# RMSNorm with SiLU on one core: rstd and gamma in one pass by rows, an even split of the squares, and no alignment of VectorE's code

## The chip, the cores and the metric

The kernel runs on one core of a Trainium2 chip. The metric is the device time of one execution in microseconds (us), as a median over runs. One more execution is taken by the hardware profiler; from it come the profile page and the trace.

## The reference

```python
x: (8, 1024, 2048) float32;  gamma: (2048,) float32;  eps = 1e-5
rms = sqrt(mean(x ** 2, axis=-1, keepdims=True) + eps)
out = gamma * x / rms
return out * (1 / (1 + exp(-out)))        # SiLU
```

So there are 8192 rows of 2048 numbers. Each row has one statistic (its root mean square), and every element is read once and written once: 67.11 MB in, 67.11 MB out.

## The kernel before

The rows are cut into 16 blocks of 512 rows. A block lies in SBUF as 128 partitions with J = 4 rows of d = 2048 each, so a block is a tile of 128x8192 float32, 4.19 MB. Six such blocks (BUFS) form a ring, `xt`; everything is computed in place in the ring. A block is loaded by one DMA that ScalarE issues (`load`, L70; blocks 4 and 5 come in one double load, L74), and stored by one DMA that SyncE issues (`store`, L146). The load of block b+6 has to wait until block b's store has emptied the buffer. That wait stands in ScalarE's own instruction stream, in front of what ScalarE does next. TensorE is used once at the start, to spread gamma over the 128 partitions.

The order of all instructions is written out by hand (`tc.manual_schedule()`). The steps of a block b are:

- `squares_scalar(b)` (L91) and `squares_vector(b)` (L100): sums of squares of the four rows. The first `share(b)` rows go to ScalarE, the others to VectorE. The share is two, but one in blocks 4, 6, 8, 10 and 12. Between ScalarE's first and second square (or behind its only one) stands a load.
- `root(b)` (L113, ScalarE) and `invert(b)` (L119, VectorE): from the sums to 1/rms (`rstd`). From block 2 on, blocks go in pairs, and one root and one reciprocal serve both (128x8). Each root costs two loads of ScalarE's function table, one for the root and one to go back to SiLU.
- `multiply(b)`: in blocks 0 and 1 (`SINGLE`), one scalar-tensor-tensor per row, which multiplies by `rstd` and gamma in one pass (L133). In all later blocks (`plain`), one tensor-tensor over the whole block that multiplies by gamma alone (L130). That one doesn't need the statistic, so it is issued right behind the block's squares.
- `silu(b)`: in blocks 0 and 1, two instructions of two rows each (L142). In later blocks, four instructions of one row, which take `rstd` as their per-partition scale (L139). Then the store.

In the main loop, for b = 2, 4, ... 14, ScalarE and VectorE do in this order: the squares of b+1 (with the load of b+3), root and reciprocal for b and b+1, the multiply of b+1, SiLU and store of b, the squares of b+2 (with the load of b+4), the multiply of b+2, SiLU and store of b+1.

At the very start VectorE has an `addr_align` to a multiple of 128 instruction slots (L151). It moves the code that follows to the next such slot, and VectorE branches over the hole.

Of the kernel before, what the change touches and what calls it, by code (L numbers as in the profile page):

```python
# [7 lines left out]
ACT = mybir.ActivationFunctionType  # L8
# [3 lines left out]
@with_exitstack  # L12
def kernel(
    ctx: ExitStack,
    tc: tile.TileContext,
    x: bass.AP,
    gamma: bass.AP,
    eps: bass.AP,
    out: bass.AP,
):  # L20

    nc = tc.nc
    P = nc.NUM_PARTITIONS
    f32 = mybir.dt.float32
    x2 = x.flatten_outer_dims()
    o2 = out.flatten_outer_dims()  # L30
    n, d = x2.shape
    J = 4
    BUFS = 6
    SLOTS = 128
    SINGLE = 2
    SHARE = {4: 1, 6: 1, 8: 1, 10: 1, 12: 1}
    nblk = n // (P * J)
    PAIRS = (4,)

    def view(t, b):  # L40

        for q in PAIRS:
            if b in (q, q + 1):
                both = t[q * P * J:(q + 2) * P * J, :].rearrange("(p j) d -> p (j d)", p=P, j=2 * J)
                return both[:, (b - q) * J * d:(b - q + 1) * J * d]
        return t[b * P * J:(b + 1) * P * J, :].rearrange("(p j) d -> p (j d)", p=P, j=J)

    singles = ctx.enter_context(tc.tile_pool(name="singles", bufs=1))
    small = ctx.enter_context(tc.tile_pool(name="small", bufs=2))
    psum = ctx.enter_context(tc.tile_pool(name="psum", bufs=1, space=bass.MemoryType.PSUM))  # L50

    Q = 4
    w = d // Q
    g = singles.tile([P, d], f32)
    eps_t = singles.tile([P, 1], f32)
    ones = singles.tile([P, P], f32)
    junk_a = psum.tile([P, d], f32, name="junk_a")
    junk_v = psum.tile([P, d], f32, name="junk_v")
    ring = singles.tile([P, BUFS * J * d], f32, name="xt")
    sss, rmss, rstds = {}, {}, {}  # L60

    def rows(b, j, k):
        at = (b % BUFS) * J + j
        return ring[:, at * d:(at + k) * d]

    def row(b, j):
        return rows(b, j, 1)

    def load(b):
        nc.scalar.dma_start(out=rows(b, 0, J), in_=view(x2, b))  # L70

    def load_pair(b):
        both = x2[b * P * J:(b + 2) * P * J, :].rearrange("(p j) d -> p (j d)", p=P, j=2 * J)
        nc.scalar.dma_start(out=rows(b, 0, 2 * J), in_=both)  # L74

    def group(b):

        return [b] if b < SINGLE else [b, b + 1]

    def sums(b):  # L80
        if b not in sss:
            k = len(group(b))
            t = small.tile([P, k * J], f32, name="ss")
            for i, m in enumerate(group(b)):
                sss[m] = (t, i * J)
        return sss[b]

    def squares_scalar(b, loads=()):
        t, at = sums(b)
        for j in range(share(b)):  # L90
            nc.scalar.activation(out=junk_a, in_=row(b, j), func=ACT.Square,  # L91
                                 accum_out=t[:, at + j:at + j + 1])
            if j == 0:
                for s in loads:
                    load(s)

    def squares_vector(b):
        t, at = sums(b)
        for j in range(share(b), J):
            nc.vector.tensor_tensor_reduce(  # L100
                out=junk_v, in0=row(b, j), in1=row(b, j), scale=1.0, scalar=0.0,
                op0=ALU.mult, op1=ALU.add, accum_out=t[:, at + j:at + j + 1])

    def share(b):
        return SHARE.get(b, 2)

    def plain(b):
        return b >= SINGLE

    def root(b):  # L110
        k = len(group(b)) * J
        rms = small.tile([P, k], f32, name="rms")
        nc.scalar.activation(out=rms, in_=sss[b][0], func=ACT.Sqrt, scale=1.0 / d, bias=eps_t)  # L113
        rmss[b] = rms

    def invert(b):
        k = len(group(b)) * J
        rstd = small.tile([P, k], f32, name="rstd")
        nc.vector.reciprocal(out=rstd, in_=rmss.pop(b))  # L119
        for i, m in enumerate(group(b)):  # L120
            rstds[m] = (rstd, i * J)

    def scale(b, j):
        t, at = rstds[b]
        return t[:, at + j:at + j + 1]

    def multiply(b):
        if plain(b):
            whole = rows(b, 0, J).rearrange("p (j d) -> p j d", j=J)
            nc.vector.tensor_mul(out=whole, in0=whole, in1=g.unsqueeze(1).to_broadcast([P, J, d]))  # L130
            return
        for j in range(J):
            nc.vector.scalar_tensor_tensor(out=row(b, j), in0=row(b, j), scalar=scale(b, j),  # L133
                                           in1=g, op0=ALU.mult, op1=ALU.mult)

    def silu(b):
        if plain(b):
            for j in range(J):
                nc.scalar.activation(out=row(b, j), in_=row(b, j), func=ACT.Silu, scale=scale(b, j))  # L139
        else:  # L140
            for h in range(0, J, 2):
                nc.scalar.activation(out=rows(b, h, 2), in_=rows(b, h, 2), func=ACT.Silu)  # L142
        store(b)

    def store(b):
        nc.sync.dma_start(out=view(o2, b), in_=rows(b, 0, J))  # L146

    with tc.manual_schedule():

        load(0)  # L150
        nc.vector.addr_align(SLOTS, max_nops=0)  # L151
        nc.vector.memset(ones, 1.0)  # L152
        nc.vector.memset(eps_t, float(eps))
        nc.scalar.activation(out=junk_a[:, 0:1], in_=ones[:, 0:1], func=ACT.Square)  # L154
        nc.sync.dma_start(out=g[0:1, :], in_=bass.AP(tensor=gamma.tensor, offset=gamma.offset, ap=[[d, 1], [1, d]]))
        for c in range(Q):
            cols = slice(c * w, (c + 1) * w)
            nc.tensor.matmul(junk_v[:, cols], ones[0:1, :], g[0:1, cols], start=True, stop=True)  # L158
        load(1)
        nc.vector.tensor_copy(out=g, in_=junk_v)  # L160
        nc.scalar.copy(out=junk_a[:, 0:1], in_=junk_v[:, d - 1:d])  # L161
        for b in range(2, PAIRS[0]):
            load(b)
        for b in PAIRS:
            load_pair(b)


        squares_scalar(0)
        squares_vector(0)
        root(0)  # L170
        invert(0)
        multiply(0)
        squares_scalar(1)
        silu(0)
        squares_vector(1)
        root(1)
        invert(1)
        multiply(1)
        squares_scalar(2)
        silu(1)  # L180
        squares_vector(2)
        multiply(2)

        for b in range(SINGLE, nblk, 2):
            squares_scalar(b + 1, [b + 3] if BUFS <= b + 1 and b + 3 < nblk else [])
            squares_vector(b + 1)
            root(b)
            invert(b)  # L190
            multiply(b + 1)
            silu(b)
            ahead = b + 2
            if ahead < nblk:
                if b == SINGLE:
                    load(BUFS)
                    silu(b + 1)
                    squares_scalar(ahead, [BUFS + 1])
                    squares_vector(ahead)
                    multiply(ahead)  # L200
                    continue
                squares_scalar(ahead, [ahead + 2] if ahead + 2 < nblk else [])
                squares_vector(ahead)
                multiply(ahead)
            silu(b + 1)


# [33 lines left out]
```

## Time and profile before

| | |
|---|---|
| median of 3 runs | 318.05 us (317.35 to 318.18) |
| the profiled execution | 317.71 us, of which the span of the profile is 315.3 us |
| VectorE (DVE) busy | 229.3 us, 73% of the span, 108 instructions |
| ScalarE (ACT) busy | 201.6 us, 64% of the span, 144 instructions |
| DMA | 134.24 MB, 426 GB/s over the span |

The span runs from the first to the last instruction of the program; 2.4 us of the execution lie around it. In the lines of the profile, `out<-in` names what an instruction writes and reads, `x` is a count, then come busy time and mean duration in nanoseconds, and then the idle time of the engine just ahead of them with what ended it. The DMA row gives the busy share of the 16 DMA engines in 40 slices of the span, in tenths. Queue q10 carries the loads, q1 the stores and the gamma row, q14 the engines' own code.

### The profile page before, as it was taken

To read this page: it belongs to the slowest core of one execution; us is meant where nothing else is said; L and a number is where in the kernel's file an instruction comes from. 1 tells how busy PE (TensorE), PEld (TensorE's weight loads), DVE (VectorE), ACT (ScalarE), POOL (GpSimd) and SP (SyncE) were. 2 spreads that over 40 slices of the span, in tenths; PEclk is the share of its full clock that TensorE was granted. 3 is DMA by queue.
4 is the path that set the end of the run, shared out by engine and by line. 5 is a ranking of instruction groups with operands and counts; after the bars stand their busy time and mean duration, and the time that the engine had idled before them with its cause. 6 is when DMAs were issued, how large, how long until landed. Compare 5 with 4: busy or idle time off the path is not lost.

```text
span 315.3 us, 398 instructions
## 1 busy us (share of the span) xinstructions
PE 7.2 (2%) x8; PEld 2.5 (1%) x8; DVE 229.3 (73%) x108; ACT 201.6 (64%) x144; POOL 0.2 (0%) x4
## 2 busy tenths in 40 slices
PE   6200000000000000000000000000000000000000
PEld 2000000000000000000000000000000000000000
DVE  0579599979797999799933999349992599891000
ACT  1249999079854993793808948098470999699100
POOL 0000000000000000000000000000000000000000
DMA  8999999999999999999999999999999999999996
GB/s 331 412 453 416 437 412 399 470 461 399 416 449 417 449 416 449 424 441 432 432 437 428 445 420 449 416 449 416 449 416 453 412 453 412 453 412 461 403 466 270
DMA packets 4468, 134.24 MB, mean 426 GB/s; under 512 B 497, under 2 KB 497, under 8 KB 497
## 3 DMA queue, kind: packets, MB, share of 16 engines
q10 hardware_dynamic: 2160, 67.11, 49.7%
q1 hardware_dynamic: 2306, 67.12, 49.3%
q14 instruction: 2, 0.02, 0.0%
HBM read 67.12 MB, written 67.11 MB: 426 GB/s over the span
## 4 chain that ended last, share of the span: by engine, by line
DMA 51%; ACT 21%; DVE 17%; issue 2%; ACTq 1%; DVEq 0%
DMA out_dram<-xt 44%; ACT xt L139 13%; DVE xt L130 8%; DMA xt<-in_x_dram 7%; DVE junk_v L100 6%; DVE xt L133 3%; ACT L113 2%; ACT junk_a L91 2%; ACT xt L142 2%; ACT L139 1%; ACTq L236 1%; ACT rms L113 0%; ACTq L70 0%; ACT L142 0%; DVE ss L100 0%
## 5 line engine op out<-in xcount | busy, mean ns | idle before, releaser
L130 DVE TENSOR_TENSOR xt<-xt,g 128x8192 f32<-128x8192 f32 x14 | 121.3, 8666 | 2.6 <-ACT junk_a L91 2.0
L139 ACT ACTIVATE xt<-xt,rstd 128x2048 f32<-128x2048 f32 x56 | 107.3, 1989 | 14.7 <-DMA out_dram<-xt 14.6
L100 DVE CUSTOM_DVE_ANT_0 junk_v<-xt 128x2048 f32<-128x2048 f32 x37 | 85.0, 2297 | 3.2 <-DMA xt<-in_x_dram 2.5
L91 ACT ACTIVATE junk_a<-xt 128x2048 f32<-128x2048 f32 x27 | 50.5, 1871 | 47.2 <-DMA out_dram<-xt 40.5
L119 DVE RECIPROCAL rstd<-rms 128x8 f32<-128x8 f32 (+1 forms) x9 | 1.8, 197 | 40.4 <-ACT rms L113 40.4
L113 ACT ACT_TABLE_LOAD x9 | 11.5, 1283 | 17.9 <-DVE ss L100 17.9
L133 DVE SCALAR_TENSOR_TENSOR xt<-xt,rstd,g 128x2048 f32<-128x2048 f32 x8 | 18.3, 2346 | 0.1
L142 ACT ACTIVATE xt<-xt 128x4096 f32<-128x4096 f32 x4 | 14.4, 3613 | 0.6 <-DVE xt L133 0.6
L139 ACT ACT_TABLE_LOAD x7 | 9.0, 1283 | 0.1
L160 DVE COPY g<-junk_v 128x2048 f32<-128x2048 f32 x1 | 2.3, 2291 | 8.1 <-PE junk_v L158 8.1
L158 PE MATMUL junk_v<-g,ones 1*128 1x512 f32 x8 | 7.2, 1072 | 2.4 <-DMA g<-in_gamma_dram 2.4
L161 ACT COPY junk_a<-junk_v 128x1 f32<-128x1 f32 x1 | 0.1, 144 | 9.4 <-DVE g L160 9.4
L100 DVE DVE_READ_ACCUMULATOR2_ANT ss<- 128x1 f32 x37 | 5.2, 141 | 0.0
L91 ACT ACTIVATION_READ_ACCUMULATOR junk_a<-xt 128x1 f32 x27 | 5.0, 186 | 0.0
L113 ACT ACTIVATE rms<-ss,eps_t 128x8 f32<-128x8 f32 (+1 forms) x9 | 2.7, 300 | 0.1
L142 ACT ACT_TABLE_LOAD x2 | 2.6, 1283 | 0.0
L158 PEld LDWEIGHTS junk_v<-g,ones 1*128 1x128 f32 x8 | 2.5, 325 | 5.5 <-issue 3.1
L154 ACT ACT_TABLE_LOAD x1 | 1.3, 1283 | 1.1 <-PEq L222 1.1
L152 DVE MEMSET ones<- 128x128 f32 x1 | 0.2, 165 | 1.4 <-PEq L222 1.4
L154 ACT ACTIVATE junk_a<-ones 128x1 f32<-128x1 f32 x1 | 0.2, 174 | 0.0
L222 POOL MEMSET const-bfloat16-1.0<- 128x1 bf16 x1 | 0.1, 102 | 0.0
L222 POOL MEMSET const-uint8-127<- 128x1 uint8 x1 | 0.1, 102 | 0.0
(3 smaller groups left out, 0.3 us busy)
## 6 DMA issues: line engine op xcount, KB each, us to landing
out_dram<-xt SPq DMA_DIRECT2D x16, 4096.0 KB, 43.3
xt<-in_x_dram ACTq DMA_DIRECT2D x14, 4096.0 KB, 26.0
g<-in_gamma_dram SPq DMA_DIRECT2D x1, 8.0 KB
xt<-in_x_dram ACTq DMA_DIRECT2D x1, 63.2
```

The costliest lines, as they stand in the source:

```text
L91: nc.scalar.activation(out=junk_a, in_=row(b, j), func=ACT.Square, accum_out=t[:, at + j:at + j + 1])
L100: nc.vector.tensor_tensor_reduce(out=junk_v, in0=row(b, j), in1=row(b, j), scale=1.0, scalar=0.0, op0=ALU.mult, op1=ALU.add, accum_out=t[: ...
L113: nc.scalar.activation(out=rms, in_=sss[b][0], func=ACT.Sqrt, scale=1.0 / d, bias=eps_t)
L119: nc.vector.reciprocal(out=rstd, in_=rmss.pop(b))
L130: nc.vector.tensor_mul(out=whole, in0=whole, in1=g.unsqueeze(1).to_broadcast([P, J, d]))
L133: nc.vector.scalar_tensor_tensor(out=row(b, j), in0=row(b, j), scalar=scale(b, j), in1=g, op0=ALU.mult, op1=ALU.mult)
L139: nc.scalar.activation(out=row(b, j), in_=row(b, j), func=ACT.Silu, scale=scale(b, j))
L142: nc.scalar.activation(out=rows(b, h, 2), in_=rows(b, h, 2), func=ACT.Silu)
L154: nc.scalar.activation(out=junk_a[:, 0:1], in_=ones[:, 0:1], func=ACT.Square)
L158: nc.tensor.matmul(junk_v[:, cols], ones[0:1, :], g[0:1, cols], start=True, stop=True)
L160: nc.vector.tensor_copy(out=g, in_=junk_v)
L236: with _tile.TileContext(nc) as tc:
```

## The change

Four things change.

- `multiply` takes the form of blocks 0 and 1 for every block: one scalar-tensor-tensor per row, by `rstd` and gamma at once. It now needs the reciprocal, so it moves: the loop does `multiply(b)` and `multiply(b + 1)` behind `invert(b)`, and the multiplies behind the squares of block 2 and of the later blocks b+2 go.
- `silu` takes the form of blocks 0 and 1 for every block: two instructions of two rows, without a scale.
- `share` is two in every block.
- The `addr_align` goes.

The pairs with one root for two blocks, the ring, the loads and the stores stay.

```diff
-    SLOTS = 128
     SINGLE = 2
-    SHARE = {4: 1, 6: 1, 8: 1, 10: 1, 12: 1}
...
     def share(b):
-        return SHARE.get(b, 2)
-
-    def plain(b):
-        return b >= SINGLE
+        return 2
...
     def multiply(b):
-        if plain(b):
-            whole = rows(b, 0, J).rearrange("p (j d) -> p j d", j=J)
-            nc.vector.tensor_mul(out=whole, in0=whole, in1=g.unsqueeze(1).to_broadcast([P, J, d]))
-            return
         for j in range(J):
             nc.vector.scalar_tensor_tensor(out=row(b, j), in0=row(b, j), scalar=scale(b, j),
                                            in1=g, op0=ALU.mult, op1=ALU.mult)

     def silu(b):
-        if plain(b):
-            for j in range(J):
-                nc.scalar.activation(out=row(b, j), in_=row(b, j), func=ACT.Silu, scale=scale(b, j))
-        else:
-            for h in range(0, J, 2):
-                nc.scalar.activation(out=rows(b, h, 2), in_=rows(b, h, 2), func=ACT.Silu)
+        for h in range(0, J, 2):
+            nc.scalar.activation(out=rows(b, h, 2), in_=rows(b, h, 2), func=ACT.Silu)
         store(b)
...
         load(0)
-        nc.vector.addr_align(SLOTS, max_nops=0)
         nc.vector.memset(ones, 1.0)
...
         squares_vector(2)
-        multiply(2)
...
             root(b)
             invert(b)
+            multiply(b)
             multiply(b + 1)
             silu(b)
             ahead = b + 2
...
                     squares_scalar(ahead, [BUFS + 1])
                     squares_vector(ahead)
-                    multiply(ahead)
                     continue
                 squares_scalar(ahead, [ahead + 2] if ahead + 2 < nblk else [])
                 squares_vector(ahead)
-                multiply(ahead)
             silu(b + 1)
```

## The prediction

> **What bounds the kernel now.** I read the page's DMA row and queues first, then its groups, then the waits, and last single stretches of the DMA view. From the page:
>
> ```profile
> PE 7.2 (2%) x8; PEld 2.5 (1%) x8; DVE 229.3 (73%) x108; ACT 201.6 (64%) x144; POOL 0.2 (0%) x4
> ...
> DMA  8999999999999999999999999999999999999996
> ...
> q10 hardware_dynamic: 2160, 67.11, 49.7%
> q1 hardware_dynamic: 2306, 67.12, 49.3%
> q14 instruction: 2, 0.02, 0.0%
> ...
> L130 DVE TENSOR_TENSOR xt<-xt,g 128x8192 f32<-128x8192 f32 x14 | 121.3, 8666 | 2.6 <-ACT junk_a L91 2.0
> L139 ACT ACTIVATE xt<-xt,rstd 128x2048 f32<-128x2048 f32 x56 | 107.3, 1989 | 14.7 <-DMA out_dram<-xt 14.6
> L100 DVE CUSTOM_DVE_ANT_0 junk_v<-xt 128x2048 f32<-128x2048 f32 x37 | 85.0, 2297 | 3.2 <-DMA xt<-in_x_dram 2.5
> L91 ACT ACTIVATE junk_a<-xt 128x2048 f32<-128x2048 f32 x27 | 50.5, 1871 | 47.2 <-DMA out_dram<-xt 40.5
> ...
> L133 DVE SCALAR_TENSOR_TENSOR xt<-xt,rstd,g 128x2048 f32<-128x2048 f32 x8 | 18.3, 2346 | 0.1
> L142 ACT ACTIVATE xt<-xt 128x4096 f32<-128x4096 f32 x4 | 14.4, 3613 | 0.6 <-DVE xt L133 0.6
> ```
>
> The 16 DMA engines are full from the first slice to the last: loads (q10) and stores (q1) take 99.0% of the span. VectorE is idle for a quarter of it, ScalarE for a third, and ScalarE's longest waits, 40.5 and 14.6 us, are for stores that must empty a ring buffer. One block is 4.19 MB in and as much out; stores alone land 9.7 us apart, a load and a store together 19.36 us apart (the chain starts ScalarE's load issues at 127.53 and 185.60, three blocks apart). A pair of blocks has 38.7 us. The kernel can only lose time where neither queue holds work, that is behind the last load, or where one DMA engine is late. The DMA view of the last store issues (stretches at 268, 285 and 292 us; KB, us to landing), and what VectorE and ScalarE do ahead of them:
>
> ```profile
> out_dram<-xt SPq DMA_DIRECT2D x1, 4096.0 KB, 26.9
> out_dram<-xt SPq DMA_DIRECT2D x1, 4096.0 KB, 19.5
> out_dram<-xt SPq DMA_DIRECT2D x1, 4096.0 KB, 21.6
> ```
>
> ```profile
> 276.27 0.20 DVE L119 RECIPROCAL rstd<-rms 128x8 f32<-128x8 f32 x1 [1.71 <-ACT rms L113]
> 276.39 8.64 DVE L130 TENSOR_TENSOR xt<-xt,g 128x8192 f32<-128x8192 f32 x1
> 277.55 15.25 ACT L139 ACTIVATE xt<-xt,rstd 128x2048 f32<-128x2048 f32 x8
> ```
>
> Stores 13, 14, 15 are issued at 268.2, 285.3, 292.8 and land at 295.1, 304.8, 314.4: the last two wait about 10 us behind their predecessors. The DMA view of 3.9 to 4.0 us, and of 313.5 to 315.3 us, shows a straggler:
>
> ```profile
> q14 instruction: 1, 0.01, 19.2%
> ```
>
> ```profile
> DMA packets 1, 0.00 MB, mean 0 GB/s; under 512 B 1, under 2 KB 1, under 8 KB 1
> ```
>
> A packet of code lies among the first load's data (19.2% of 16 engines in 0.1 us is 0.31 us). At the end 15 of 16 engines have sent their completion by 313.4; one sends its own at 314.1, 0.7 us later. That engine is already 0.8 us late when the first load completes.
>
> **The change part by part.** *VectorE, a pair of blocks.* Out go two L130 (17.3 us) and, in most pairs, five squares; in come eight row multiplies of the L133 form and four squares. Eight rows at the pitch of L133 (four take 9.14 us) are 18.2 us, four squares with their accumulator reads 9.5, reciprocal 0.2: 28 of 38.7 us. *ScalarE.* Eight L139 (15.9 us) become four L142 (14.5); squares go from three to four (3.9 us a two); two table loads and the root stay, 2.9: 25.2 us. Neither engine becomes the bound.
>
> The Trainium skill (Vector Engine (DVE) Microarchitecture Reference, Points that are easy to get wrong) says that scalar-tensor-tensor with two SBUF sources that aren't bf16 runs at half rate. By it a row would take twice L130's 2.17 us; the eight L133 rows here, fp32 from SBUF, took 2.35.
>
> *The chain inside a pair.* Gamma no longer goes in ahead of the statistics, so SiLU of block b waits for two row multiplies, then for four. Counted from load b+3's issue: square, root and reciprocal until 4.2, rows 1 and 2 until 8.8, SiLU's half until 12.5, rows 3 and 4 until 13.4, second half and store b at 17.0 (before: 13.0, 127.53 to 140.54). ScalarE squares two rows of b+2 around the wait for load b+4 (19.4), VectorE ends block b+1 at 22.6, store b+1 goes at 29.1 (before 27.4). ScalarE is at load b+5 by 31, due at 38.7. So stores go 2 to 4 us later out of the 43 to 50 us that they spend queued, and loads go when they did. The queues stay full, and the order in them (SP's 16 stores, ScalarE's loads) is the old one: 0. ScalarE's waits for stores shrink by about what its new waits for L133's successor add.
>
> *The ramp.* Blocks 0 and 1 are unchanged. Store 2 goes about 71 instead of 75.8 us, load 6 up to 3 us later than 68.1 (ScalarE's queue stands before it at a SiLU), covered by the double load that lands at 76.1; load 8 about 109.8 instead of 108.2, covered by load 7 until 114.8. 0.
>
> *The tail.* From load 15's issue (243.66), with rows of this trace: reciprocal 247.7, rows of 12 and 13 until 257.0 and 266.1, squares of 14 and 15 until 270.8 and 275.6 on VectorE; ScalarE sends store 12 at 260.7 and 13 at 271.7, squares of 15 until 275.5, root 277.3. Rows of 14 then end at 286.6 and of 15 at 295.7, SiLU's second halves at 290.3 and 299.4: stores 14 and 15 go 5.0 and 6.6 us later. What cover is left? Most engines finish a store about 1.4 us before it lands (313.0 to 313.4 against 314.4), so store 14 must bring packets by 293.7 and 15 by 303.4. The first load bounds the lead: issue at 0.73, first packets from 1.74, each then 1.9 us instead of 1.2: 1.7 us. That leaves 1.7 us at store 14 and 2.3 at store 15, price 0. The other bound is the first store: issued at 35.99, first packet at 40.7, behind load packets. Were 4.7 us needed here too, the engines would idle 1.4 us. I take 0, the stretch behind the loads having no load packets to stand behind.
>
> *The code's place.* Without the alignment VectorE's branch at L151 (0.76 us, next instruction only at 1.39) goes; the 0.6 us lie beside the gamma row's DMA (2.3): 0. With it should go the code packet at 3.95, since that branch alone jumps to another stretch of code. VectorE then runs on to the next stretch in mid-kernel, with 140 instructions (64 row multiplies, 32 squares and 32 reads, 9 reciprocals, 3 others) instead of 108, and a packet comes there. The packet at 102.4 us, another engine's, took 0.31 us and nobody waited. The late engine gets back 0.85 us (0.31, and by the trace's packets 1.75 instead of 1.21 for the data packet behind it) and pays 0.31: -0.5. Bounds: -0.7, where the other 15 end, and +0.3, if nothing goes and one comes. I take -0.5, by these two packets.
>
> The Trainium skill (Runtime: NRT & Kernel Launch, Instruction fetch mechanics) says that a taken branch out of the loaded window stalls for its code, while running over a boundary is mostly hidden. The two packets agree; by it alone the sum is the same.
>
> *Sum.* The profiled execution is 317.7, 0.3 under the median of 318.05. 317.7 - 0.5 = 317.2, as a median 317.5.
>
> **Rivals.** *The packet stays or comes back as dear elsewhere* (the alignment doesn't do what I say): 318.05. For it: no view names the packet's owner. *The tail's cover runs out (slower).* Place: the rows of 14 and 15 behind the last root. It decides once a wait on that chain is over 1.7 us, or the lead is nearer 4.7. Price: 1.4 for the lead gives 318.05 - 0.5 + 1.4 = 318.9; a wait for code of up to 3.2 us (branch 0.76 to packet 3.95) in that stretch gives 318.05 - 0.5 + 3.2 - 1.7 = 319.0; both, 322.1. I price it 319.5. Against it: ScalarE ran over its own boundary without a gap. *More comes back than the packet*: all of the 0.7 and 0.4 from the spread of runs (317.35 to 318.18), 316.9. *Half-rate rows, VectorE the bound*: a pair takes 8 x 4.33 + 9.7 = 44.3 us, 5.6 more in each of seven, 357. The L133 rows speak against it.
>
> **How the numbers follow.** Forecast 0.62, packet stays 0.13, tail 0.19, more back 0.05, half rate 0.01. A measurement of this kernel can tell about 0.3%, 0.95 us: faster is under 317.1, slower over 319.0. Of the forecast 0.03 lies below 317.1. So faster 0.08, same 0.72, slower 0.20. The range runs from 316.9 (the -0.7 and the spread) to 319.6, into the tail rival.
>
> **What would show it.** Right: DMA row full, no code packet before 5 us and one in mid-kernel, stores 14 and 15 issued near 290 and 299 and still landing 9.7 us apart, ScalarE's waits for stores shorter and a new wait of SiLU on the row multiplies. Wrong: a slice under 9 before the last, landings further apart than 9.7 us behind the last load, a row multiply over 2.4 us, or a gap on VectorE that no semaphore ends.

## The result, and the profile after

The kernel after took 316.78 us in the median of 6 runs (316.57 to 317.4), the kernel before beside it 317.94 (317.35 to 318.18). The ratio is 0.9968, with a 95% interval of 0.9955 to 0.9980: faster by 0.6 to 1.4 us, which is about the 0.3% above which a difference can be told from none. The profiled execution took 316.85 us with a span of 315.1. From the page of the kernel after:

```profile
PE 7.2 (2%) x8; PEld 2.5 (1%) x8; DVE 224.6 (71%) x140; ACT 204.6 (65%) x126; POOL 0.2 (0%) x4
...
DMA  8999999999999999999999999999999999999996
...
q10 hardware_dynamic: 2160, 67.11, 49.8%
q1 hardware_dynamic: 2306, 67.12, 49.4%
q14 instruction: 2, 0.02, 0.0%
...
L124 DVE SCALAR_TENSOR_TENSOR xt<-xt,rstd,g 128x2048 f32<-128x2048 f32 x64 | 145.6, 2345 | 0.3
L129 ACT ACTIVATE xt<-xt 128x4096 f32<-128x4096 f32 x32 | 115.0, 3611 | 35.9 <-DVE xt L124 35.9
L89 ACT ACTIVATE junk_a<-xt 128x2048 f32<-128x2048 f32 x32 | 59.9, 1873 | 45.8 <-DMA out_dram<-xt 41.2
```

The DMA row is the same, full up to the last slice. VectorE lost 4.7 us of busy time and ScalarE gained 3.0, and neither shows in the end. SiLU has its new wait, 35.9 us on the row multiplies, and ScalarE's waits for stores shrank from 55 to 41 us. The row multiply took 2.35 us. The timeline of the kernel after, behind the last root:

```profile
277.64 0.20 DVE L114 RECIPROCAL rstd<-rms 128x8 f32<-128x8 f32 x1 [1.71 <-ACT rms L108]
277.88 18.19 DVE L124 SCALAR_TENSOR_TENSOR xt<-xt,rstd,g 128x2048 f32<-128x2048 f32 x8
282.53 3.62 ACT L129 ACTIVATE xt<-xt 128x4096 f32<-128x4096 f32 x1 [3.62 <-DVE xt L124]
287.06 3.62 ACT L129 ACTIVATE xt<-xt 128x4096 f32<-128x4096 f32 x1 [0.91 <-DVE xt L124]
291.58 3.62 ACT L129 ACTIVATE xt<-xt 128x4096 f32<-128x4096 f32 x1 [0.91 <-DVE xt L124]
296.11 3.62 ACT L129 ACTIVATE xt<-xt 128x4096 f32<-128x4096 f32 x1 [0.91 <-DVE xt L124]
```

ScalarE's SiLU waits each time for its two rows, 0.91 us. Stores 14 and 15 go at 290.7 and 299.7 us, 5.4 and 6.9 us later than before. The DMA view of the kernel after at these issues (stretches at 272, 290 and 299 us) gives their landings:

```profile
out_dram<-xt SPq DMA_DIRECT2D x1, 4096.0 KB, 22.8
out_dram<-xt SPq DMA_DIRECT2D x1, 4096.0 KB, 13.9
out_dram<-xt SPq DMA_DIRECT2D x1, 4096.0 KB, 14.5
```

They land at 294.9, 304.6 and 314.2, still 9.7 us apart. The code packets have moved. The DMA view of 0 to 6 us has no line of q14 any more:

```profile
q10 hardware_dynamic: 49, 1.61, 72.3%
q1 hardware_dynamic: 2, 0.01, 0.9%
```

The stretches of 84 to 85 and of 99 to 100 us have one code packet each (a share of 1.9% of 16 engines in 1 us is 0.31 us):

```profile
q14 instruction: 1, 0.01, 1.9%
```

### The profile page after: what moved, and what is told of

Read it like the earlier page. It is cut to its first block, busy times and chain, and to the rows that moved or that the text cites. A ratio compares the mean times of both kernels' runs of the same rounds, so it can differ in the third digit from the quotient of the medians.

```text
span 315.1 us, 402 instructions
## 1 busy us (share of the span) xinstructions
PE 7.2 (2%) x8; PEld 2.5 (1%) x8; DVE 224.6 (71%) x140; ACT 204.6 (65%) x126; POOL 0.2 (0%) x4
## 4 chain that ended last, share of the span: by engine, by line
DMA 51%; DVE 22%; ACT 18%; issue 3%; DVEq 1%; ACTq 0%
DMA out_dram<-xt 44%; DVE xt L124 20%; ACT xt L129 10%; DMA xt<-in_x_dram 7%; ACT junk_a L89 5%; DVE junk_v L98 2%; ACT L108 2%; DVEq L220 1%; ACT rms L108 0%; ACTq L68 0%; ACT L129 0%; DVE rstd L114 0%; DVE ss L98 0%; ACT L140 0%; ACTq L108 0%
## 5 line engine op out<-in xcount | busy, mean ns | idle before, releaser
L124 DVE SCALAR_TENSOR_TENSOR xt<-xt,rstd,g 128x2048 f32<-128x2048 f32 x64 | 145.6, 2345 | 0.3
L129 ACT ACTIVATE xt<-xt 128x4096 f32<-128x4096 f32 x32 | 115.0, 3611 | 35.9 <-DVE xt L124 35.9
L89 ACT ACTIVATE junk_a<-xt 128x2048 f32<-128x2048 f32 x32 | 59.9, 1873 | 45.8 <-DMA out_dram<-xt 41.2
L98 DVE CUSTOM_DVE_ANT_0 junk_v<-xt 128x2048 f32<-128x2048 f32 x32 | 73.5, 2298 | 1.5 <-DMA xt<-in_x_dram 0.7
L89 ACT ACTIVATION_READ_ACCUMULATOR junk_a<-xt 128x1 f32 x32 | 6.0, 186 | 0.0
L98 DVE DVE_READ_ACCUMULATOR2_ANT ss<- 128x1 f32 x32 | 4.5, 140 | 0.0
```

What stands on the lines that cost most here:

```text
L98: nc.vector.tensor_tensor_reduce(out=junk_v, in0=row(b, j), in1=row(b, j), scale=1.0, scalar=0.0, op0=ALU.mult, op1=ALU.add, accum_out=t[: ...
```

## The experiments

**The code's place alone, from both sides.** First the kernel before without the alignment:

```diff
-        nc.vector.addr_align(SLOTS, max_nops=0)
```

> The kernel before, with the alignment of VectorE's code taken out and nothing else changed. Theory P (the place of the code is all of the gain: no packet of code among the first load's data, and less time around the span): about 316.8 us, like the kernel after (316.78), with the first code packet in mid-kernel and 1.8 us instead of 2.4 us between span and execution. Theory W (the gain comes from the changed work, rows in one pass and squares two and two): about 317.9 us, like the kernel before. A third, that ScalarE's smaller number of instructions shortens the end: the span falls by 0.2 to 0.3, but 2.4 us stay around it, so about 317.6.

Measured: 316.79 us (316.72 to 317.36), ratio to the kernel before 0.9979 (0.9971 to 0.9988). Spans lie at 314.9 in the median, 1.9 us lie around them; in the runs of the kernel before beside it, spans lie at 315.3 and 2.3 us around them. The code packets came at 103.7 and 120.6 us, none near 4. All of the old work, and the time of the kernel after: theory P.

Then the kernel after with the alignment:

```diff
+        nc.vector.addr_align(128, max_nops=0)
         nc.vector.memset(ones, 1.0)
```

> The kernel after, with the alignment to a multiple of 128 slots put back and nothing else changed. Theory P: about 317.9 us, like the kernel before (317.94), with a code packet again near 4 us and 2.4 us around the span. Theory W: about 316.8 us. With 140 instead of 108 VectorE instructions behind the aligned slot, a further stretch of code is reached inside the kernel; if that is waited for in the last pair of blocks, up to 1 us more.

Measured: 317.81 us (317.26 to 318.6), ratio 1.0006 (0.9995 to 1.0017). The new work with the old alignment has the old time, theory P again, but by another sum. Only 1.8 us lie around the span here, not the 2.4 that were expected, and the span grew, from 315.0 to 316.0 in the median. Its DMA view of the stretch behind 313.5 us:

```profile
DMA packets 4, 0.03 MB, mean 12 GB/s; under 512 B 3, under 2 KB 3, under 8 KB 3
...
q1 hardware_dynamic: 4, 0.03, 2.9%
```

Four packets, one of them with 32 KB of data: one engine is still moving data when the others have sent or are sending their completion. This kernel has three code packets, at 4.0, 101.2 and 235.7 us. No view names a packet's engine. The one near 100 us comes when ScalarE has begun 63 to 67 instructions, in this kernel as in the others, wherever VectorE's code lies; so the first and the last are put down to VectorE. The last completion came at 315.05, against 313.9 in the kernel after.

**A branch that stays in its stretch of code.**

```diff
+        nc.vector.addr_align(128, offset=100, max_nops=0)
         nc.vector.memset(ones, 1.0)
```

> The kernel after with VectorE's code moved to slot 100 of 128 instead of slot 0, so that it branches over a hole as the kernel before does, but probably inside the stretch of code that it is in. Theory P in the form that the packet counts (a jump to another stretch fetches the next one early): no code packet before 5 us, one in mid-kernel earlier than at 84 us, about 316.8 us. If the branch as such costs, whatever its target: 317.3 to 317.9 us. Theory W: 316.8 us, and the packets don't matter.

Measured: 317.04 us (316.69 to 317.45), ratio 0.9977 (0.9968 to 0.9986). VectorE still branches at 0.75 us, its next instruction stands at 1.02 (1.39 in the kernel before, 0.82 without a branch), and no packet comes before 53 us. Spans are 315.0, and 2.0 us lie around them (1.8 to 2.2 in single runs), which is why the time lies 0.3 us over the kernel after. So the branch by itself is harmless to the span; the packet that comes early with the other branch is what the span pays for. The timeline of VectorE in this kernel, its first line:

```profile
1.02 0.17 DVE L139 MEMSET ones<- 128x128 f32 x1 [1.02 <-PEq L207]
```

The Trainium skill (Runtime: NRT & Kernel Launch, Instruction fetch mechanics) says that running over a boundary of code is mostly hidden, and that a taken branch out of the window stalls for its code. On the first the traces agree: VectorE has no idle time at the packets in mid-kernel. A stall for code no run here shows: from branch to next instruction it takes 0.6 us where the branch leaves the stretch and 0.27 us where it stays, but no code packet lies between the two. The early one comes at 3.95 us, 2.6 us after that next instruction has begun.

**No computation.** Squares, roots, multiplies and SiLU are left out, and each block is stored as it was loaded. What stands in place of the loop:

```diff
+        for b in range(nblk):
+            store(b)
+            if b + BUFS < nblk:
+                load(b + BUFS)
```

> Only the loads and stores: squares, roots, multiplies and SiLU are left out, blocks are stored as they were loaded, through the same ring and queues. Theory that the DMA engines bound both kernels: 316 to 317 us, at most 1 us less than the kernel after, since 32 transfers of 9.7 us and the same start and end are left. If the engines' work sets more of the time than the DMA row tells: 310 us or less.

Measured: 316.71 us (316.47 to 316.81), ratio 0.9970 (0.9959 to 0.9982). From its page:

```profile
PE 7.2 (2%) x8; PEld 2.5 (1%) x8; DVE 2.5 (1%) x3; ACT 1.6 (1%) x3; POOL 0.2 (0%) x4
...
DMA  8999999999899999999999999999999999999997
```

VectorE and ScalarE do nothing, the DMA row is what it was, and the time is that of the kernel after. All that could still be gained at the computation is some 0.1 us, less than can be told.

**The tail's cover.** Squares whose result is not used, between the last reciprocal and the rows of block 14 (`idle_squares` runs VectorE's square of a row k times; k = 1, 2, 4):

```diff
             invert(b)
+            if b == nblk - 2:
+                idle_squares(b, k)
             multiply(b)
```

> The kernel after, with one square more on VectorE (its result is not used) between the last reciprocal and the row multiplies of block 14, so that stores 14 and 15 go 2.4 us later, near 293.1 and 302.1 us. How long ahead of its predecessor's end must a store be issued? Lead of 1.7 us, as the prediction took it from the first load: cover of about 1.2 us at store 14, so 1.2 us more than the kernel after, 318.0. No lead needed: still covered, 316.8. A lead of 4.7 us (first store): 2.4 us or more on top, 319.2.

> The same with two squares more, 4.8 us. Lead of 1.7 us: 3.6 us more than the kernel after, 320.4. No lead needed: 1.9 us more, 318.7. A lead of 4.7 us: 4.8 us or more on top, 321.6.

> The same with four squares more, 9.6 us. Beyond the cover every microsecond counts, so 4.8 us more than with two squares: 325.2 with a lead of 1.7 us, 323.5 with none, 326.4 with 4.7 us. If less than 4.8 us is added between two and four, the cover isn't what ends.

Measured: 316.89 (316.64 to 317.26), 318.29 (317.39 to 319.26) and 322.56 us (321.95 to 323.14, four runs). One square is free, two cost 1.4 us, four cost 5.7. That is nearest to "no lead needed", and better than it. The DMA view at store 14's issue, with two squares and with four, has the same line (issue at 294.9 and 298.6):

```profile
out_dram<-xt SPq DMA_DIRECT2D x1, 4096.0 KB, 11.1
```

```profile
DMA packets 0, 0.00 MB, mean 0 GB/s; under 512 B 0, under 2 KB 0, under 8 KB 0
...
out_dram<-xt SPq DMA_DIRECT2D x1, 4096.0 KB, 11.1
```

The second fence is the stretch of 294.5 to 299 us with four squares: no packet at all, the DMA engines are idle. A store that finds them idle takes 11.1 us from issue to landing; one that queues lands 9.7 us behind its predecessor. So the lead is 11.1 - 9.7 = 1.4 us ahead of the predecessor's landing. Of this, 0.8 us pass from the issue to the first packet: in the traces with two and with four squares, the first packet of store 14 stands at 295.7 and 299.4. In the kernel after store 13 lands at 294.9, store 14 may go until 293.5 and goes at 290.7: 2.8 us of cover. With one square it goes at 293.5, at that point (in its own trace store 13 lands at 295.3, so that some 0.4 us are left), and with two 1.4 us behind it, which is what the run lost.

Between two and four squares the medians grew by 4.3 us, and less than 4.8 was named as a sign that it isn't the cover that ends. The profiled executions answer that. There the last root came 1.1 us earlier with four squares than with two, store 14 went 3.7 us later, and the time grew by 3.7 us (318.31 to 322.01). So beyond the cover every microsecond counts.

**Work in mid-kernel.** Two such squares in each pair from block 4 to block 12:

```diff
             invert(b)
+            if SINGLE < b < nblk - 2:
+                idle_squares(b, 2)
             multiply(b)
```

> The kernel after, with two squares more on VectorE (results not used) at the same place in each of the five pairs from block 4 to block 12, 24 us of VectorE work on the chain from reciprocal to store. Theory that the DMA engines bound every pair: no change, 316.8 (up to 0.4 more for a further packet of code). If VectorE or the chain through it bounds a pair: up to 24 us more, 341; if the loads come too late behind ScalarE, some microseconds.

Measured: 317.32 us (317.11 to 317.65), 0.4 us over the kernel with one square in the tail, beside which it ran. 24 us more on VectorE's chain cost half a microsecond, and that in the tail: the late pair 12 moves the last root to 280.4 (277.3 in the kernel after), store 14 goes at 293.8, 0.5 us past its point (store 13 lands at 294.7 there), and the DMA view at that issue has the same 11.1 us line as above. The packets of code came at 81.9 and 96.4, none more than in the kernel after. In mid-kernel the added work is free.

**What lies around the span.** The kernel before once more, and once with VectorE's code 16 slots further:

```diff
-        nc.vector.addr_align(SLOTS, max_nops=0)
+        nc.vector.addr_align(SLOTS, offset=16, max_nops=0)
```

> The kernel before once more, unchanged, for the span of each of its runs. Theory L (its 2.4 us around the span belong to where VectorE's code ends, slot 249 of a stretch of 256): 2.4 us around the span in every run, against 1.75 to 1.81 in the kernel after; 317.6 to 317.9 us. If the 2.4 us were one run's chance: 1.8 us in most.

> The kernel before with VectorE's code 16 slots further (slot 16 of 128 instead of 0), so that it branches into the same stretch but runs over that stretch's end inside the kernel and not behind it. Theory L: 1.8 us around the span; the early packet near 4 us stays and a third comes near 260 us, each 0.3 us on the late DMA engine, so a span near 315.6 and about 317.4 us. If the branch or the early packet makes the 2.4 us: 2.4 us around the span, about 318.0 us.

Measured, unchanged: 317.4 us (317.1 to 318.26), 2.3 to 2.4 us around the span in every run, spans 315.0 in the median. 16 slots further: 317.74 us (317.51 to 318.03), ratio to the kernel before 1.0009 (1.0000 to 1.0018). 1.9 us lie around the span, and spans are 315.8, with code packets at 3.9, 102.8 and 265.7. The time lies between the two forecasts (317.4 and 318.0), so its parts have to decide. Theory L holds in its direction: the 2.4 us belong to where VectorE's code lies, neither to the branch nor to the early packet, which are both still there. The other half of it holds in size: the span grows by 0.8. That the third packet falls to the engine that is late already is inferred: at the end a single completion, at 314.77, lies 1.0 us behind the last but one.

## Why the prediction was right or wrong

Right: what bounds the kernel. The computation's worth is nothing, as the runs without any of it and with 24 us more of it show. The changed work alone (the kernel after against the kernel before without alignment, 316.78 and 316.79) moved nothing that can be told; these are two sets of runs, and their ratios to the kernel before beside each, 0.9968 and 0.9979, have intervals that overlap.

Right: the engines' own terms. Row multiplies at 2.35 us, eight in 18.19 (worked out: 18.2), the new wait of SiLU, ScalarE's shorter waits for stores. Stores 14 and 15 were put at 290.3 and 299.4 and went at 290.7 and 299.7. The chain inside a pair held to within a microsecond or two.

Right, but over-careful: the tail. The prediction took 1.7 us of lead, from the first load, on top of the 1.4 us by which most engines end ahead of a landing, and had 1.7 us of cover left at store 14. The runs show 0.8 us from issue to first packet, and that 1.4 us in all ahead of the predecessor's landing is enough (that this equals the prediction's other 1.4, which holds 0.7 us of the late engine, is chance): 2.8 us of cover. The bound of 4.7 us, from the first store, was the wait behind load packets and no lead. So the rival on the slower side was further off than it was priced: its mechanism exists (two squares more make it visible), and the change stays 2.8 us short of it.

Right in place, mis-sized: the early code packet. It went, one came in mid-kernel, and one engine was no longer late. At the start the 0.85 us are there: the first load lands at 13.7 to 13.8 us in the four traces with an early packet, at 12.9 to 13.1 in those of the other kernels that compute. At the end less is left. The sum booked -0.5. The spans fell by 0.1 to 0.3: medians of 315.1 to 315.3 in three sets of runs of the kernel before (21 to 29 each), 315.0 in the kernel after; where the alignment alone goes, side by side, they fell by 0.4. With the straggler gone, others set the end: in the kernel after four engines finish between 313.6 and 313.9, where the kernel before had 15 of them done by 313.4. The DMA view of the kernel after from 313.5 to 315 us, where the kernel before has one packet:

```profile
DMA packets 4, 0.00 MB, mean 0 GB/s; under 512 B 4, under 2 KB 4, under 8 KB 4
```

Of a branch that stalls for its code the prediction said that the trace's two packets agree. That was too much. The packet at 3.95 came long after the branch's next instruction had begun (1.39), so it doesn't show a branch that waits for code; why that branch brings the packet early isn't shown either.

Wrong: the last step, "317.7 - 0.5 = 317.2". It carried the 2.4 us between span and execution over unchanged. They became 1.75 to 1.81, -0.55 us. That is about half of the measured gain of 1.16 us; where the alignment alone goes, it is 0.42 of 0.82 us. It is the same edit, the alignment, but another mechanism than the packet, and no view of the page shows it, since it lies behind the last instruction of the program. The forecast of 317.5 was 0.7 us too high, and the measured 316.78 lies 0.1 under the low end of its range (set at 316.9 against a kernel before of 318.05; beside the kernel after it took 317.94). Against the larger sets of the kernel before (317.5 to 317.6) the kernel after gained 0.7 to 0.8 us, near the forecast -0.5, but that is in part luck: the packet was booked too high and the time around the span not at all, and the two errors offset each other. By the ratio the gain stands at 0.32%, with the 0.3% inside its interval, where the prediction held most of its chance within 0.3%.

What stays open: which engine waits behind the span in the kernel before, and for what. The trace's semaphore records there show one step of 0.51 us, 1.7 to 2.2 us behind the span, in both traces of this kernel. It takes 0.10 us in the kernel after and in every other kernel here; against the kernel after, the other steps are alike to 0.02 us. That moving VectorE's code by 16 slots takes it away is shown. That VectorE runs over the end of its stretch just then is only a guess, and the records don't bear it out: behind the span of the kernel before they hold no code packet. The kernel with offset 100 has one there, at 316.74 us, and its step is 0.10.

## What to carry to other kernels

Where the DMA row is full from end to end, take the computation out once: the time that is left says what all further work on the computation can gain (here 0.1 us). What remained here were the late one of 16 DMA engines and the time outside the span, so compare execution less span before comparing spans. Ahead of the end, price a delayed store by the time that a lone store takes against the distance of two queued ones, here, for stores of 4.19 MB, 11.1 against 9.7 us: it is free as long as it is issued by that difference ahead of its predecessor's landing.

## What the runs showed of the hardware that was not expected

- An alignment of code can cost in two places at once: about 0.85 us of one DMA engine for a packet of code that arrives among the first data (the packet itself takes 0.31, here as in mid-kernel), and 0.55 us behind the program's last instruction. In the kernel after, moved from slot to slot, execution less span was 1.8 us in the median unaligned, 1.8 aligned and 2.0 at offset 100.
- Two code packets of VectorE seem to count together: with both, the span grew by 1.0 us over the same kernel without alignment, and by 0.8 in the kernel with 16 slots. In both traces a single completion comes 1.0 us behind the last but one (0.7 and 0.3 in the two traces of the kernel before), and the last store has landed only with the last of 16. That both packets fall to one DMA engine is inferred from this.
- A whole store into idle DMA engines takes 11.1 us for 4.19 MB, in two kernels, and in a third where 11 engines were still at their last packets; that is only 1.4 us more than its share in a full queue.
